# Four feed-forward gemms begun with half-token products, their first weights summed and split in the output projection, norm sums on VectorE

## The chip, the cores and the metric

One core of one Trainium2 chip runs the whole program. The metric is the device time of one execution in microseconds, as the median of several executions; lower is better. The profile is one execution of the same program, with its own time.

## The reference

One decoder layer over 1024 tokens of width 1024, in float32. After three token mixers (not touched here) it does

```python
x = x + mixed @ w_out                      # output projection
h = rms_norm(x, norm2_g)
ff = silu(h @ w_gate) * (h @ w_up)         # 1024 -> 2816, twice
x = x + ff @ w_down                        # 2816 -> 1024
x = x + sigmoid(x @ ple_gate) * (p @ ple_proj)
return rms_norm(x, final_g)
```

`rms_norm` divides each token by the root of its mean square, so h of a token is known only when all 1024 outputs of the output projection are known for that token.

## The kernel before, in words

Activations lie transposed: features on the 128 partitions, 512 tokens (a half) along the free axis. A "unit" is a tile of 128x512. Every float32 product is made of three TensorE products: each operand is split into a rounded high part (a copy on ScalarE, `act.copy`) and a rest (a subtraction on VectorE), and hi·hi, hi·lo and lo·hi are summed in PSUM.

**Output projection** (loop before the feed forward): for each token half `hf`, eight gemms of 24 matmuls; `out_evac` adds the residual on VectorE, squares on ScalarE, and sums the squares on VectorE. `norm2(hf)` follows its half: matmuls with a column of ones (`rstd`), a power on GpSimd, a matmul that spreads the result over the partitions (`rows`), then `normed` scales the eight units. `norm2(0)` runs beside the gemms of the second half; `norm2(1)` can begin only after the last gemm.

**Feed forward.** 22 gemms (gate and up for each of 11 pairs of 128-feature blocks), each by the Winograd form of Strassen's scheme: the output is 2 feature blocks x 2 token halves, and seven products of 12 matmuls stand in for eight. The token operands of the seven are B[0] to B[6]. B[0] and B[1] are the split normed units of the first half. B[2] to B[6] need the second half: per k of four, `T1 = t12 - ts0`, `T2 = t22 - T1`, B[2] = T2, B[3] = t22 - t12, B[4] = T1, B[5] = t22, B[6] = t21 - T2. In `norm2` the subtractions of T1 and T2 stand on VectorE, those of B[3] and B[6] on GpSimd; each B unit is then split by `b_split` (one copy on ScalarE, one subtraction on VectorE). The B units stay on the chip for all 22 gemms. The weight operands are sums of four blocks (`pool.tensor_tensor`, four per gemm, on GpSimd), split by `act.copy` and `vec.tensor_tensor` in `weights()`.

The order within a gemm is fixed in `Gemm`: `head1` (product 0, into bank X, then copied to p1 by ScalarE), `head2` (product 1), `middle` (products 2, 3, 4; X is copied as u after product 2 and as v after product 4 by ScalarE, and product 4 waits until u is read), `tail1` (product 5 on top of X, which waits until v is read), `tail2` (product 6). The heads of the next gemm are put between the tails of the current one. `op_slots` lets six split weight operands be ready ahead; two gemms' raw weights are held (`raw_slots`), in `stg` and in `ffp`, and `down_sums` has two tiles "dr" of its own for the down projection's weights, which it sums on GpSimd and stores.

`weights()` is started at the last-but-one gemm of the output projection (`j == KT - 2`).

**Down projection.** 77 steps of 12 matmuls; `d_load` loads two units a step, four steps ahead (`d_slots`), and `d_split` splits both. They are started after the last feed-forward gemm has been issued.

**What sets the order.** All engines execute their instructions in program order. `Flow` is a planner in Python: it keeps an estimated clock, advanced by the matmuls issued (`fl.tick`), and generators started with `fl.spawn` issue their instructions when their estimated due time comes. A wait (`yield`, `Event`, `Slots`) in the planner decides where an instruction stands in its engine's queue; on the chip the instruction waits for its data and for its buffer only. GpSimd's cost in the planner does not depend on what VectorE does, and VectorE's not on GpSimd.

Of the kernel before, what the change touches and what calls it, by code (L numbers as in the profile page):

```python
# [9 lines left out]
F32 = mybir.dt.float32  # L10
# [6 lines left out]
P = 128  # L17
S = 1024
HALF = 512
D = 1024  # L20
# [175 lines left out]
def kernel(  # L196
# [1020 lines left out]

    B = [[None] * 4 for _ in range(7)]
    B_ev = [[Event(fl) for _ in range(4)] for _ in range(7)]

    def b_split(i, k, t, sub):
        hi, lo = B[i][k] = unit(F32R), unit(F32R)
# [5 lines left out]
    def norm2(hf, ts):  # L1228
# [19 lines left out]
        for k in range(4):  # L1248
            t12, t22 = normed(k), normed(4 + k)
            T1[k], T2[k] = unit(), unit()  # L1250
            vec.tensor_tensor(out=T1[k], in0=t12, in1=ts[0][k], op=ALU.subtract)
            yield fl.lag("vec")
            vec.tensor_tensor(out=T2[k], in0=t22, in1=T1[k], op=ALU.subtract)
            ts[0][k] = None
            fl.spawn(b_split(2, k, T2[k], vec), fl.left())
            yield fl.lag("vec")
        for k in range(4):
            t = ts[1][k]
            pool.tensor_tensor(out=t, in0=ts[1][4 + k], in1=t, op=ALU.subtract)
            fl.spawn(b_split(3, k, t, vec), fl.left())  # L1260
            ts[1][k] = None
            yield 0.7
        for k in range(4):
            fl.spawn(b_split(4, k, T1[k], vec))
            T1[k] = None
            yield 1.3
        for k in range(4):
            t = ts[0][4 + k]
            pool.tensor_tensor(out=t, in0=t, in1=T2[k], op=ALU.subtract)
            fl.spawn(b_split(5, k, ts[1][4 + k], vec))  # L1270
            T2[k] = ts[1][4 + k] = None
            yield 1.3
        for k in range(4):
            fl.spawn(b_split(6, k, ts[0][4 + k], vec))
            ts[0][4 + k] = None
            yield 1.3

# [4 lines left out]
    jobs = []  # L1282
    for p in range(NPR):
        jobs += [(w_gate[2 * p], w_gate[2 * p + 1]), (w_up[2 * p], w_up[2 * p + 1])]
    ops, op_free = [], []
    op_slots, raw_slots = Slots(fl, 6), Slots(fl, 2)
    op_n = [0]

    def op_tile():
        n = op_n[0] % 6  # L1290
        op_n[0] += 1
        hp, tag = ((stg, "wh"), (stg, "wl"), (ffp, "op"))[n % 3]
        t = hp.tile([P, 8, P], F32R, tag=tag, name=nm("op"))
        return t[:, 0:4], t[:, 4:8]

    def weights():
        loaded = []

        def loader():
            for sa, sb in jobs:  # L1300
                yield from raw_slots.take()
                ra = stg.tile([P, KT, P], F32, tag="wr", name=nm("wr"))
                rb = ffp.tile([P, KT, P], F32, tag="wr", name=nm("wr"))
                ev = Event(fl)
                sync.dma_start(out=rb, in_=sb)
                sync.dma_start(out=ra, in_=sa)
                loaded.append((ra, rb, ev))
                ev.set(3.6)
                more.append(0)
                if waiting:  # L1310
                    waiting.pop().set()
                yield 0.1

        more, waiting = [], []
        fl.spawn(loader())
        own = []

        uses = [(0, 0), (0, 1)]
        for n in range(len(jobs)):
            uses += [(n, 2), (n, 3), (n, 4), (n + 1, 0), (n, 5), (n + 1, 1), (n, 6)]  # L1320
        for n, i in uses:
            if n == len(jobs):
                continue
            if n == len(own):
                if not more:
                    waiting.append(Event(fl))
                    yield waiting[-1]
                more.pop()
                ra, rb, ev = loaded.pop(0)
                yield ev  # L1330
                a11, a12, a21, a22 = ra[:, 0:4], ra[:, 4:8], rb[:, 0:4], rb[:, 4:8]
                s1 = unit(shape=(P, 4, P))
                pool.tensor_tensor(out=s1, in0=a21, in1=a22, op=ALU.add)
                pool.tensor_tensor(out=a21, in0=a11, in1=a21, op=ALU.subtract)
                own.append((a11, a12, a11, a21, s1, a12, a22))
                ra = rb = s1 = None
            yield from op_slots.take()
            a11, a12, s2, s3, s1, s4, a22 = own[n]
            if i == 2:
                pool.tensor_tensor(out=s2, in0=s1, in1=a11, op=ALU.subtract)  # L1340
                pool.tensor_tensor(out=s4, in0=a12, in1=s2, op=ALU.subtract)
            raw = own[n][i]
# [3 lines left out]
            ops.append((hi, lo))  # L1346
            if op_free:
                op_free.pop().set()
            if i == 6:
                own[n] = None  # L1350
                raw_slots.give()
            yield 0.3

    def next_op():
# [15 lines left out]


    class Gemm:
        def __init__(self, done):
            self.done = done

            self.read = {n: Event(fl) for n in ("p1", "u", "v", "y")}

# [10 lines left out]
        def middle(self):  # L1388
            fl.until(self.read["p1"])
            product(self.X, 2, False, True)  # L1390
            fl.spawn(self.snap("u"), 0.3)
            self.Y = bank(True)
            product(self.Y, 3, True, True)
            fl.until(self.read["u"])
            product(self.X, 4, False, True)
            fl.spawn(self.c22(), 0.3)

        def tail1(self):
            fl.until(self.read["v"])
            product(self.X, 5, False, True)  # L1400
            fl.spawn(self.done(self.X, None, 0, 1), 0.3)

        def tail2(self):
            fl.until(self.read["y"])
# [3 lines left out]
        def snap(self, name):  # L1408
            t = unit()
            setattr(self, name, t)  # L1410
            act.copy(out=t, in_=self.X)
            self.read[name].set()
            yield 0

# [57 lines left out]

    def down_sums(p):

        da, db = (ffp.tile([P, D], F32, tag="dr", name=nm("dr")) for _ in range(2))
        sync.dma_start(out=da, in_=w_down[2 * p])
        sync.dma_start(out=db, in_=w_down[2 * p + 1])
        s1 = unit()
# [6 lines left out]
        yield fl.lag("pool")  # L1485
        for i, t in enumerate((a11, a21, s1, a12)):
            sync.dma_start(out=wd_d[i, p], in_=t)

    xl_load(0)
    ts2 = [[None] * KT, [None] * KT]  # L1490
    for hf in range(2):
# [15 lines left out]
    todo = []  # L1507
    for p in range(NPR):
        ts, ev = [[None, None], [None, None]], Event(fl, 4)
        todo += [(p, Gemm(gate_done(ts)), None), (p, Gemm(up_done(ts, ev)), (ts, ev))]  # L1510
    todo[0][1].head1()
    todo[0][1].head2()
    for n, (p, g, ab) in enumerate(todo):
        g.middle()
        nxt = todo[n + 1][1] if n + 1 < len(todo) else None
        if nxt:
            nxt.head1()
        g.tail1()
        if nxt:
            nxt.head2()  # L1520
        g.tail2()
        if ab:
            fl.spawn(a_sums(p, *ab), 0.4)
        else:
            fl.spawn(down_sums(p), 2.0)
    B = None

    x2 = [[None] * KT, [None] * KT]  # L1530
# [19 lines left out]
    def d_split():  # L1550
        for _ in steps_:
# [10 lines left out]
            if d_wait:  # L1562
                d_wait.pop().set()
            yield 0.3

    def down_evac(ps, j, hf, last, read):
        vec.tensor_tensor(out=x1[hf][j], in0=ps, in1=x1[hf][j], op=ALU.add)
# [36 lines left out]
            fl.tick(3 * T_R)  # L1604
        d_slots.give()

    fl.spawn(d_load())
    fl.spawn(d_split(), 0.1)
    fl.tick(0.6)
    ff.close()  # L1610
    wd = ctx.enter_context(tc.tile_pool(name="wd", bufs=4))
# [176 lines left out]
```

## Time and profile before

| | us |
|---|---|
| median of 3 runs | 1272.01 (1271.91 to 1272.81) |
| the profiled execution | 1270.8 |
| its span, first to last instruction | 1268.8 |
| TensorE busy | 1219.7 (96%) |
| VectorE busy | 796.7 (63%) |
| ScalarE busy | 522.0 (41%) |
| GpSimd busy | 326.8 (26%) |

In the profile, PE is TensorE's matmuls, DVE is VectorE, ACT ScalarE, POOL GpSimd, SP the queue that issues the DMAs. Busy shares are averages over stages that differ; the strip of 40 slices and the tables by stretch show where a stage departs from them. Tiles are named without numbers: `mm` and `dn` are PSUM banks, `u` a unit, `op` a split weight operand, `wr` raw weights, `dr` raw weights of the down projection, `x_d` and `a_d` scratch in DRAM.

### The profile page before, as it was taken

What the parts mean: (1) busy time and instruction counts of PE and PEld (TensorE: products, weight loads), DVE (VectorE), ACT (ScalarE), POOL (GpSimd) and SP (SyncE); (2) the same over time, 40 slices, a digit from 0 to 9 for tenths busy, and PEclk for the clock granted to TensorE, in tenths of its full rate; (3) what the DMA queues carried; (4) which work ended last, traced back from release to release, by engine and by line L of the source; (5) the groups of instructions that cost most, each with busy time, mean ns of one, the idle gap of its engine ahead of it and who ended that gap; (6) DMA issues with size and microseconds to landing.
All of it is one profiled execution on the core that took longest, in us unless ns stands there. A gap on an engine that the chain in (4) does not pass through costs nothing.

```text
span 1268.8 us, 17177 instructions
## 1 busy us (share of the span) xinstructions
PE 1219.7 (96%) x6151; PEld 1006.5 (79%) x6151; DVE 796.7 (63%) x1361; ACT 522.0 (41%) x1102; POOL 326.8 (26%) x265
## 2 busy tenths in 40 slices
PE   7999999999999994999999999999989999999996
PEld 5778888888877872788888888888867888888896
DVE  8674886975675678756555555654447555574573
ACT  7266344253244342433333333333326542454442
POOL 7100000100100025456666655666310000000000
PEclk9999999999999995899999999999999999999998
DMA  6056254232245551145345545345578565562241
GB/s 221 17 154 190 86 134 121 101 84 84 100 158 160 189 191 50 57 151 184 108 156 191 166 149 182 112 156 199 191 277 293 193 199 172 161 215 67 84 144 57
DMA packets 105157, 187.18 MB, mean 148 GB/s; under 512 B 22960, under 2 KB 34032, under 8 KB 105072
## 3 DMA queue, kind: packets, MB, share of 16 engines
q1 hardware_dynamic: 105072, 186.09, 45.0%
q8 instruction: 48, 0.79, 0.3%
q14 instruction: 37, 0.30, 0.1%
HBM read 135.95 MB, written 50.10 MB: 147 GB/s over the span
## 4 chain that ended last, share of the span: by engine, by line
PE 62%; DVE 4%; DMA 2%; ACT 1%; issue 1%; POOL 0%; SPq 0%; POOLq 0%; DVEq 0%; ACTq 0%
PE dn L346 40%; PE mm L346 22%; DVE u L140 4%; ACT u L140 1%; DMA u<-x_d 1%; DMA u<-in_w_down_dram 1%; DVE op L140 1%; DMA a_d<-u 0%; DVE wl L140 0%; ACT op L140 0%; ACT wh L140 0%; SPq L240 0%; POOL rs L140 0%; POOL wr L140 0%; POOLq L1783 0%
## 5 line engine op out<-in xcount | busy, mean ns | idle before, releaser
L346 PE MATMUL dn<-u,op 128*128 128x512 f32 x1584 | 374.8, 396 | 16.6 <-DVE u L140 9.0
L346 PEld LDWEIGHTS dn<-u,op 128*128 128x128 f32 x1584 | 300.8, 191 | 88.1 <-DVE u L140 14.7
L346 PE MATMUL mm<-u,wh 128*128 128x512 f32 x1104 | 352.2, 400 | 7.5 <-DVE u L140 6.0
L346 PEld LDWEIGHTS mm<-u,wh 128*128 128x128 f32 x1104 | 201.3, 189 | 50.9 <-DVE u L140 8.4
L140 DVE TENSOR_TENSOR u<-u,u 128x512 fp32r<-128x512 f32 (+2 forms) x330 | 219.1, 706 | 30.3 <-ACT u L140 24.2
L346 PE MATMUL mm<-u,wl 128*128 128x512 f32 x552 | 216.1, 391 | 0.2 <-DVE wl L140 0.2
L140 DVE TENSOR_TENSOR op<-wr,op 128x512 fp32r<-128x512 f32 x132 | 139.4, 1059 | 117.4 <-ACT op L140 116.9
L140 ACT CAST u<-u 128x512 fp32r<-128x512 f32 x218 | 126.0, 619 | 145.7 <-DVE u L140 72.7
L346 PE MATMUL dn<-u,u 128*128 128x512 f32 (+2 forms) x850 | 161.7, 338 | 5.9 <-DVE u L140 4.9
L346 PEld LDWEIGHTS dn<-u,u 128*128 128x128 f32 (+1 forms) x850 | 124.5, 171 | 31.4 <-DVE u L140 5.6
L140 ACT CAST op<-wr 128x512 fp32r<-128x512 f32 x132 | 81.8, 621 | 155.2 <-POOL wr L140 58.1
L346 PE MATMUL mm<-u,u 128*128 128x512 f32 (+1 forms) x618 | 123.7, 340 | 0.0
L140 POOL TENSOR_TENSOR u<-u,u 128x512 f32<-128x512 f32 (+1 forms) x69 | 99.2, 1452 | 88.8 <-DVE u L140 80.7
L346 PEld LDWEIGHTS mm<-u,wl 128*128 128x128 f32 x552 | 103.8, 188 | 23.0 <-DVE wl L140 1.0
L140 ACT ACTIVATE u<-u 128x512 f32<-128x512 f32 (+1 forms) x137 | 82.1, 605 | 78.8 <-DVE u L140 77.0
L140 DVE TENSOR_TENSOR wl<-wr,wh 128x512 fp32r<-128x512 f32 (+2 forms) x96 | 68.3, 714 | 69.4 <-ACT wh L140 68.8
L140 POOL TENSOR_TENSOR rs<-ms,mhalf 128x4 f32<-128x4 f32 (+1 forms) x7 | 6.5, 926 | 399.4 <-DVE ms L140 399.4
L346 PEld LDWEIGHTS mm<-u,u 128*128 128x128 f32 x618 | 97.4, 190 | 13.4 <-ACT u L140 0.2
L140 ACT COPY u<-dn 128x512 f32<-128x512 f32 (+4 forms) x107 | 52.4, 490 | 129.6 <-PE dn L346 129.6
L140 DVE TENSOR_TENSOR u<-dn,u 128x512 f32<-128x512 f32 x81 | 55.6, 688 | 63.7 <-PE dn L346 53.1
L140 DVE TENSOR_TENSOR u<-mm,u 128x512 f32<-128x512 f32 x64 | 43.9, 687 | 56.5 <-PE mm L346 56.5
L140 ACT CAST wh<-wr 128x512 fp32r<-128x512 f32 (+2 forms) x96 | 57.6, 607 | 24.0 <-PE mm L346 11.7
(166 smaller groups left out, 1170.1 us busy)
## 6 DMA issues: line engine op xcount, KB each, us to landing
a_d<-u SPq DMA_DIRECT2D x77, 256.0 KB, 6.1
u<-a_d SPq DMA_DIRECT2D x77, 256.0 KB, 3.3
wr<-in_w_gate_dram SPq DMA_DIRECT2D x22, 512.0 KB, 4.4
wr<-in_w_up_dram SPq DMA_DIRECT2D x22, 512.0 KB, 4.6
dr<-in_w_down_dram SPq DMA_DIRECT2D x22, 512.0 KB, 6.1
u<-wd_d SPq DMA_DIRECT2D x44, 256.0 KB, 2.7
wr<-in_w_in_dram SPq DMA_DIRECT2D x21, 512.0 KB, 3.6
wd_d<-dr SPq DMA_DIRECT2D x33, 256.0 KB, 6.0
```

What stands on the lines that cost most here:

```text
L140: return f(*a, **kw)
L346: pe.matmul(out=out, lhsT=lhsT, rhs=rhs, start=start, stop=stop, **kw)
```

## The change

- `EARLY = 4`: the first four gemms (gate and up of the first two pairs) are taken in two pairs. First come products 0 and 1 of all four, then products 2 to 6 of gemms 0 and 1 in turn, then of gemms 2 and 3. The others keep their order.
- An early gemm adds product 1 onto product 0 in the same bank X and evacuates it at once; it begins X anew with product 2, and adds p1 when it reads X: u and v become additions on VectorE (before: copies on ScalarE), and the last read of X has an addition more.
- `weights()` starts at gemm `j == 1` of the second half of the output projection. The first four operands have tiles in `ffp`; the next ones take the tiles of the output projection's weights, after `out_w` at `j == KT - 2`. Eight operand tiles then (before: six). Sums are a generator of their own per gemm. The operands 2 to 6 of a gemm wait in the planner for `t2_ev`, set when the last T2 has been issued.
- The second raw tile of a gemm and the two tiles of `down_sums` come from one set of four (before: two and two).
- The subtractions of B[3] and B[6] go from GpSimd to VectorE, in order B[2], B[3], B[4], B[5], B[6], each loop pacing itself by VectorE's queue.
- The store of x1 is planned 3 us later; `d_load` and `d_split` are started before the last gemm (before: after it).

```diff
-        yield fl.left()
+        yield fl.left() + 3.0
         sync.dma_start(out=x1_d[hf, j], in_=x)
...
+        t2_ev.set()
         for k in range(4):
             t = ts[1][k]
-            pool.tensor_tensor(out=t, in0=ts[1][4 + k], in1=t, op=ALU.subtract)
+            vec.tensor_tensor(out=t, in0=ts[1][4 + k], in1=t, op=ALU.subtract)
             fl.spawn(b_split(3, k, t, vec), fl.left())
...
         for k in range(4):
             t = ts[0][4 + k]
-            pool.tensor_tensor(out=t, in0=t, in1=T2[k], op=ALU.subtract)
-            fl.spawn(b_split(5, k, ts[1][4 + k], vec))
+            vec.tensor_tensor(out=t, in0=t, in1=T2[k], op=ALU.subtract)
+            fl.spawn(b_split(6, k, t, vec), fl.left())
...
+    EARLY = 4
+    uses = []
+    for n in range(0, EARLY, 2):
+        uses += [(n, 0), (n + 1, 0), (n, 1), (n + 1, 1)]
+    for n in range(0, EARLY, 2):
+        uses += [(n + b, i) for i in range(2, 7) for b in range(2)]
...
-    op_slots, raw_slots = Slots(fl, 6), Slots(fl, 2)
+    op_slots, ra_slots, rb_slots, out_w = Slots(fl, 4), Slots(fl, 2), Slots(fl, 4), Event(fl)
...
+            todo = [(n, c) for n in range(2) for c in range(2)] + [(2, 0), (3, 0), (2, 1), (3, 1)]
+            todo += [(n, c) for n in range(4, len(jobs)) for c in range(2)]
+            for n, c in todo:
+                if n >= 2 and c == 0:
+                    yield out_w
+                    yield from ra_slots.take()
+                else:
+                    yield from rb_slots.take()
+                fetch(n, c)
...
+                if i == 2:
+                    yield t2_ev
+                yield sum_ev[n]
...
         def head2(self):
+            if self.early:
+                fl.until(self.read["p1"])
+                product(self.X, 1, False, True)
+                fl.spawn(self.done(self.X, None, 0, 0), 0.3)
+                return
...
+            if self.early and name != "p1":
+                vec.tensor_tensor(out=t, in0=self.X, in1=self.p1, op=ALU.add)
+            else:
+                act.copy(out=t, in_=self.X)
...
-        da, db = (ffp.tile([P, D], F32, tag="dr", name=nm("dr")) for _ in range(2))
+        yield from rb_slots.take()
+        yield from rb_slots.take()
+        da, db = (raw_tile(ffp).rearrange("p k c -> p (k c)") for _ in range(2))
...
-            if hf == 1 and j == KT - 2:
+            if hf == 1 and j == 1:
                 fl.spawn(weights())
...
+            if hf == 1 and j == KT - 2:
+                out_w.set()
+                for _ in range(4):
+                    op_slots.give()
...
+    for n in range(0, EARLY, 2):
+        for f in (Gemm.head1, Gemm.head2):
+            f(g[n])
+            f(g[n + 1])
+    for n in range(0, EARLY, 2):
+        for f in (Gemm.p6, Gemm.p7, Gemm.p5, Gemm.tail1, Gemm.tail2):
+            f(g[n])
+            f(g[n + 1])
...
+        if not nxt:
+            fl.spawn(d_load())
+            fl.spawn(d_split(), 0.1)
```

In the new code `p6`, `p7` and `p5` are products 2, 3 and 4, the three parts of the old `middle`.

## Rows read from the trace of the kernel before

**Rows 1.** The page's strip of 40 slices: busy tenths, and the granted clock
```profile
PE   7999999999999994999999999999989999999996
PEclk9999999999999995899999999999999999999998
```

**Rows 2.** Table by stretch: busy us (instructions) of each engine, granted clock, DMA share
```profile
468.10:540.05 71.95, 51.02 (x170) 34.93 (x170) 54.80 (x67) 26.35 (x48) 33.95 (x23) 0.74 0.17 59
500.00:510.00 10.00, 5.74 (x12) 2.67 (x11) 9.06 (x8) 4.22 (x8) 8.69 (x7) 0.50 0.57 210
516.00:517.00 1.00, 1.00 (x6) 0.81 (x5) 0.00 (x0) 0.94 (x2) 0.00 (x0) 1.00 0.00 0
600.00:700.00 100.00, 100.00 (x443) 82.81 (x442) 54.83 (x64) 36.56 (x64) 59.81 (x43) 1.00 0.46 155
```

**Rows 3.** Timeline of PE: start, us, count, [idle before <-releaser]
```profile
468.16 2.88 PE L346 MATMUL dn<-u,op 128*128 128x512 f32 x12
470.88 2.88 PE L346 MATMUL mm<-u,op 128*128 128x512 f32 x12
476.46 1.02 PE L346 MATMUL dn<-ones,u 128*128 128x1 f32 x8 [2.70 <-DVE u L140]
479.83 2.04 PE L346 MATMUL dn<-u,ones 128*128 128x512 f32 x2 [2.35 <-DVE u L140]
485.40 0.77 PE L346 MATMUL dn<-u,op 128*128 128x512 f32 x1 [3.52 <-issue]
...
503.57 3.33 PE L346 MATMUL dn<-u,op 128*128 128x512 f32 x6 [2.95 <-DVE u L140]
```

**Rows 4.** Timeline of DVE over the same stretch
```profile
467.22 1.23 DVE L140 TENSOR_TENSOR op<-wr,op 128x512 fp32r<-128x512 f32 x1 [1.83 <-ACT op L140]
...
472.65 0.68 DVE L140 TENSOR_TENSOR u<-mm,u 128x512 f32<-128x512 f32 x1
...
481.92 1.41 DVE L140 SCALAR_TENSOR_TENSOR u<-u,vt,dn 128x512 f32<-128x512 f32 x2 [2.23 <-PE dn L346]
...
501.75 9.69 DVE L140 TENSOR_TENSOR u<-u,u 128x512 fp32r<-128x512 f32 x7
...
512.39 1.89 DVE L140 TENSOR_TENSOR u<-u,u 128x512 fp32r<-128x512 f32 x3
```

**Rows 5.** Table by stretch: the output projection of the second half
```profile
424.00:468.10 44.10, 44.10 (x198) 36.30 (x197) 30.92 (x51) 17.63 (x31) 6.70 (x6) 1.00 0.63 209
```

**Rows 6.** Groups by line and form, 545 to 900 us: count | busy, mean ns
```profile
L140 DVE TENSOR_TENSOR op<-wr,op 128x512 fp32r<-128x512 f32 x113 | 121.5, 1077 | 100.7 <-ACT op L140 100.2
L140 DVE TENSOR_TENSOR u<-dn,u 128x512 f32<-128x512 f32 x46 | 31.6, 687 | 18.3 <-PE dn L346 18.0
L140 POOL TENSOR_TENSOR wr<-wr 128x512 f32<-128x512 f32 x19 | 24.5, 1292 | 1.5
```

**Rows 7.** Timeline of PE at the entry of the down projection
```profile
928.99 3.58 PE L346 MATMUL dn<-u,u 128*128 128x512 f32 x8 [4.67 <-DVE u L140]
...
953.35 0.50 PE L346 MATMUL dn<-u,u 128*128 128x512 f32 x1 [1.02 <-ACT u L140]
```

**Rows 8.** Timeline of DVE there
```profile
924.13 0.69 DVE L140 TENSOR_TENSOR u<-dn,u 128x512 f32<-128x512 f32 x1 [2.03 <-PE dn L346]
924.85 7.69 DVE L140 TENSOR_TENSOR u<-u,u 128x512 f32<-128x512 f32 x9
```

**Rows 9.** Table by stretch, after that entry
```profile
930.00:940.00 10.00, 10.00 (x41) 8.13 (x40) 3.87 (x7) 1.24 (x2) 0.00 (x0) 0.89 0.99 352
940.00:950.00 10.00, 10.00 (x46) 8.29 (x45) 4.05 (x6) 3.63 (x6) 0.00 (x0) 1.00 1.05 385
```

**Rows 10.** The page's DMA issues: count, KB, us from issue to landing
```profile
wr<-in_w_gate_dram SPq DMA_DIRECT2D x22, 512.0 KB, 4.4
dr<-in_w_down_dram SPq DMA_DIRECT2D x22, 512.0 KB, 6.1
wd_d<-dr SPq DMA_DIRECT2D x33, 256.0 KB, 6.0
```

More of the change, by code (lines that the diff above doesn't have):

```diff
@@ L1284 @@
         jobs += [(w_gate[2 * p], w_gate[2 * p + 1]), (w_up[2 * p], w_up[2 * p + 1])]
+    EARLY = 4
[4 more added lines that the diff above has]
+        uses += [(n + b, i) for i in range(2, 7) for b in range(2)]
+    uses += [(EARLY, 0), (EARLY, 1)]
+    for n in range(EARLY, len(jobs)):
+        more = n + 1 < len(jobs)
+        uses += [(n, 2), (n, 3), (n, 4)] + [(n + 1, 0)] * more + [(n, 5)] + [(n + 1, 1)] * more + [(n, 6)]
@@ L1294, in op_tile, with raw_tile @@
         return t[:, 0:4], t[:, 4:8]
+    def raw_tile(hp):
+        return hp.tile([P, KT, P], F32, tag="wr", name=nm("wr"), bufs=2 if hp is stg else 4)
     def weights():
-        loaded = []
-        def loader():
[L1300 to L1311, printed above, removed]
-                yield 0.1
@@ L1314, in weights, with fetch @@
-        more, waiting = [], []
+        raws = [[None, None, Event(fl), Event(fl)] for _ in jobs]
+        def fetch(n, c):
+            raws[n][c] = raw_tile(ffp if c or n < 2 else stg)
+            sync.dma_start(out=raws[n][c], in_=jobs[n][c])
+            raws[n][2 + c].set(3.6)
+        def loader():
+            todo = [(n, c) for n in range(2) for c in range(2)] + [(2, 0), (3, 0), (2, 1), (3, 1)]
[7 more added lines that the diff above has]
+                fetch(n, c)
+                yield 0.1
@@ new lines, in sums @@
+        def sums(n):
+            yield raws[n][2]
+            yield raws[n][3]
+            ra, rb = raws[n][0:2]
+            a11, a12, a21, a22 = ra[:, 0:4], ra[:, 4:8], rb[:, 0:4], rb[:, 4:8]
+            s1 = unit(shape=(P, 4, P))
+            pool.tensor_tensor(out=s1, in0=a21, in1=a22, op=ALU.add)
+            pool.tensor_tensor(out=a21, in0=a11, in1=a21, op=ALU.subtract)
+            own[n] = (a11, a12, a11, a21, s1, a12, a22)
+            yield split_ev[n]
+            pool.tensor_tensor(out=a11, in0=s1, in1=a11, op=ALU.subtract)
+            pool.tensor_tensor(out=a12, in0=a12, in1=a11, op=ALU.subtract)
+            sum_ev[n].set()
@@ L1315, in weights @@
+        own = [None] * len(jobs)
+        split_ev, sum_ev = events(len(jobs)), events(len(jobs))
         fl.spawn(loader())
[L1316 to L1320, printed above, removed]
+        started = 0
         for n, i in uses:
[L1322 to L1336, printed above, removed]
-            yield from op_slots.take()
[L1338 to L1342, printed above, removed]
@@ L1343, in weights @@
+            while started < len(jobs) and started <= n + 1:
+                fl.spawn(sums(started))
+                started += 1
+            yield from op_slots.take()
+            if i < 2:
+                yield raws[n][2]
+                raw = raws[n][0][:, 4 * i:4 * i + 4]
+            else:
+                if i == 2:
+                    yield t2_ev
+                yield sum_ev[n]
+                raw = own[n][i]
             hi, lo = op_tile()
@@ L1346, in weights @@
             ops.append((hi, lo))
+            if i == 1:
+                split_ev[n].set()
             if op_free:
@@ L1349, in weights @@
             if i == 6:
-                own[n] = None
-                raw_slots.give()
+                own[n] = raws[n] = raw = None
+                (rb_slots if n < 2 else ra_slots).give()
+                rb_slots.give()
             yield 0.3
@@ L1372, with __init__ @@
     class Gemm:
-        def __init__(self, done):
-            self.done = done
+        def __init__(self, done, early=False):
+            self.done, self.early = done, early
             self.read = {n: Event(fl) for n in ("p1", "u", "v", "y")}
@@ L1386, in head2, with p6, p7, p5 @@
             fl.spawn(self.c11(), 0.3)
-        def middle(self):
+        def p6(self):
             fl.until(self.read["p1"])
-            product(self.X, 2, False, True)
+            if self.early:
+                self.X = bank(True)
+            product(self.X, 2, self.early, True)
             fl.spawn(self.snap("u"), 0.3)
+        def p7(self):
             self.Y = bank(True)
             product(self.Y, 3, True, True)
+        def p5(self):
             fl.until(self.read["u"])
@@ L1400, in tail1 @@
             product(self.X, 5, False, True)
-            fl.spawn(self.done(self.X, None, 0, 1), 0.3)
+            fl.spawn(self.done(self.X, self.p1 if self.early else None, 0, 1), 0.3)
         def tail2(self):
@@ L1410, in snap @@
             setattr(self, name, t)
-            act.copy(out=t, in_=self.X)
+            if self.early and name != "p1":
+                vec.tensor_tensor(out=t, in0=self.X, in1=self.p1, op=ALU.add)
+            else:
+                act.copy(out=t, in_=self.X)
             self.read[name].set()
@@ L1487, in down_sums @@
             sync.dma_start(out=wd_d[i, p], in_=t)
+        rb_slots.give()
+        rb_slots.give()
     xl_load(0)
@@ L1564, in d_split, with after @@
             yield 0.3
+    todo = []
+    for p in range(NPR):
+        ts, ev = [[None, None], [None, None]], Event(fl, 4)
+        early = 2 * p < EARLY
+        todo += [(p, Gemm(gate_done(ts), early), None), (p, Gemm(up_done(ts, ev), early), (ts, ev))]
+    def after(n):
+        p, _, ab = todo[n]
+        if ab:
+            fl.spawn(a_sums(p, *ab), 0.4)
+        else:
+            fl.spawn(down_sums(p), 2.0)
+    g = [t[1] for t in todo]
+    for n in range(0, EARLY, 2):
[6 more added lines that the diff above has]
+            f(g[n + 1])
+        after(n)
+        after(n + 1)
+    g[EARLY].head1()
+    g[EARLY].head2()
+    for n in range(EARLY, len(g)):
+        nxt = g[n + 1] if n + 1 < len(g) else None
+        if not nxt:
+            fl.spawn(d_load())
+            fl.spawn(d_split(), 0.1)
+        g[n].p6()
+        g[n].p7()
+        g[n].p5()
+        if nxt:
+            nxt.head1()
+        g[n].tail1()
+        if nxt:
+            nxt.head2()
+        g[n].tail2()
+        after(n)
+    B = None
     def down_evac(ps, j, hf, last, read):
@@ L1605, in down_step @@
         d_slots.give()
-    fl.spawn(d_load())
-    fl.spawn(d_split(), 0.1)
     fl.tick(0.6)
```

43 lines of the change are left out of this document (12 added, 31 removed).

## The prediction, made before the changed kernel was run

> **What bounds the kernel now.** I read the page's strip first. TensorE is at nine tenths or more nearly everywhere, so a gain can come only from slices where it is not. The deepest inner one is slice 15 (476 to 507 us), the entry of the feed forward, and there the granted clock falls too; a shallower one is slice 29, the entry of the down projection [rows 1]. The first slice and the last are not touched by the change.
>
> Next the table by stretch. A saturated feed forward runs 443 matmuls in 100 us, 0.2257 us each, with VectorE at 55% and GpSimd at 60%: more work on either there costs nothing as long as TensorE is not kept waiting. From 468.10 (the end of the output projection) to 540.05, where TensorE has been back at that pace for 12 us, 71.95 us hold 170 matmuls, 10 of them the norm's. The other 160 are worth 36.1 us, so **35.8 us are lost here**, part of it to waiting and part to the clock, which stands at 0.50, the 1.2 GHz level, in 500 to 510 and is back at 1.00 only by 516 [rows 2].
>
> The timeline of TensorE shows why. Two half-token products (2.72 us from start to start) are all it has; then come the norm's matmuls at 476.46 and 479.83, the first matmul that needs the second half at 485.40, and B[3] at 503.57 [rows 3]. VectorE's timeline names the delays. At 467.22 it sits in its queue behind a weight split that waits for ScalarE (itself late for GpSimd's sums), so the last gemm, done at about 468.4, is evacuated only at 472.65. The scaling begins at 481.92. Subtractions of two SBUF operands take 9.69 us for 7 (one per 1.4 us) in 501 to 511 while GpSimd is 87% busy, against 1.89 us for 3 (0.605 from start to start) when it is idle [rows 2, 4].
>
> **The change part by part.**
>
> *Six more half-token products.* Eight products of 2.72 us keep TensorE busy for 21.7 us after 468.2, plus the norm's matmuls: 2.0 us at full clock (1.02 and half of the 2.04, which ran at half clock [rows 3]). With 1.5 us for the norm's two waits (bounds 0 and the 5.1 of the two idle times in rows 3), product 2 could start at 493.4.
>
> *When B[2] is there.* With the first sums and splits moved some 30 us earlier, the last evacuation no longer stands behind them: 468.4 instead of 472.65, and the norm's first matmul follows at about 471, not 476.46 (evacuation, square and sum, 0.7 us each, and one split in between). From that matmul to the first scaling it took 5.46 us (476.46 to 481.92), so scaling starts at 476.5. Four times two scalings (1.32) and three subtractions (0.605 each, GpSimd idle) are 12.5 us; one evacuation between (0.69) and two of the four late weight splits bring the last T2 to 491. The first operand of product 2 is split behind it: 492.5. So TensorE, not the norm, is last here, or nearly so; I take product 2 at 494 and 0.6 us of waiting, bounds 0 and 5 (the norm chain of before kept, 4.2 us later). Queued behind that wait is all of TensorE's later work.
>
> *The sums moved into the output projection.* There TensorE never waits, VectorE is busy 30.9 of 44.1 us and GpSimd 6.7 [rows 5]. Four splits (2.4 us; three of them stood there already) and four more GpSimd sums fit under the gemms: 0. Raw weights land in 4.4 us [rows 10], with DMA at 0.63. If the cover were gone (VectorE late for the weights of the next gemm), it would cost up to 2 us. The later x1 store holds only a buffer longer; behind it on SP stand the loads of the early weights, needed tens of us later: 0.
>
> *The two pairs.* Every B stage now feeds two products, 5.4 us of TensorE. From 491 to the use of the last B[6] tile (494 + 8 products 21.7 + 2 = 518) VectorE has 27 us. Its work: 24 instructions for B[3] to B[6] (8 subtractions, now its own, and 16 splits), 10 weight splits, all 0.605, and 10 evacuations and snapshots at 0.687 [rows 6]: 20.6 + 6.9 = 27.5. Beside it GpSimd makes the eight sums of gemms 2 and 3, since their second raw tiles can land only after the sixth operand of gemms 0 and 1 is split (slots), at about 503. A VectorE instruction beside GpSimd took 1.45 us on average against 0.605, 0.85 more; eight of them, 6.8. So VectorE needs 34.3 us for 27: **7.3 us of waiting**, spread over B[4] to B[6]. Bounds: 0, if the sums fall where VectorE has evacuations from PSUM, and 14. The moved subtractions add 8 x 0.605 = 4.8 us to VectorE and spare it 8 x 0.85 = 6.8 of waiting behind GpSimd; the copies taken from ScalarE gain nothing, as ScalarE is not last. Gemms 2 and 3 find all of B there: 0.5 (0 to 3).
>
> Lost after: 2.0 + 1.5 + 0.6 + 7.3 + 0.5 = 11.9. Gain at this entry 35.8 - 11.9 = **23.9** (bounds 13 and 33).
>
> *Down projection.* TensorE stands 4.67 us at its entry, since the splits of the first steps lie in VectorE's queue behind the last evacuation at 924.13 [rows 7, 8], and then has 41 matmuls in 10 us instead of 44.3 (clock 0.89), 0.75 us more [rows 9]. With `d_load` and `d_split` before the last gemm the splits lie beside that gemm: up to 5.4 us gained. But DMA is at 0.99 to 1.05 for the 20 us behind, and already made step 8 wait at 953.35; a TensorE that starts sooner gets there sooner. I take **3**, bounds 0 and 6. The added risk: a copy that waits for a landing stands ahead of the last gemm's snapshots on ScalarE.
>
> *The rest.* Eight operand tiles and the shared raw tiles: 0 in a saturated stretch (priced as a rival below).
>
> **Sum.** 1270.8 (span 1268.8 and 2.0 around it) - 23.9 - 3.0 = 1243.9. The median of before is 1.2 above its profiled execution, so the forecast is **1245**, its own range 1238 to 1254.
>
> **Where a page bears on it.** VectorE's splits (both inputs in SBUF) average 1.077 us in the feed forward, its evacuations from PSUM 0.687, beside the same GpSimd [rows 6]. The Trainium skill, page "SBUF — State Buffer", section "Who interferes with whom", says that a VectorE instruction with two SBUF inputs and a GpSimd instruction that reads SBUF exclude each other for the whole instruction, while one with a single SBUF input is not disturbed. The trace agrees in kind. By that rule each of the eight sums could hold VectorE for its full length, and the moved subtractions are put on the engine that is held; this is worked out from rows as rival A.
>
> **Rivals.**
>
> *A: VectorE becomes the bound and the clock falls again.* The eight sums cost VectorE their whole 1.292 us [rows 6], 10.3 instead of 6.8; TensorE, fed a tile at a time, drops to 0.50 as it did around 500 to 510 [rows 2], and some 30 matmuls at half clock cost 0.2257 more each, 6.8. The gain at the down projection is eaten by DMA, 3.0. Together 13.3: 1258. For it: the same feeding by tiles before. Against: TensorE has 21.7 us of full work just ahead and two products per stage.
>
> *B: no stall in the pairs.* The sums find VectorE in evacuations or come after the B stages: 7.3 less, and the down projection gives 5: 1236. Against: VectorE's own 27.5 us already fill its 27.
>
> *C: the raw tiles become the wait (slower).* `down_sums` now takes two of four tiles that gemms need for the second half of their weights. It holds them for the load (6.1), four sums (5.2 to 6.5) and the stores (6.0), some 18 us of a pair's 38 [rows 6, 10]. If a gemm's load came last behind these stores, the nine later pairs would each wait. It turns slower from 27 / 9 = 3 us a pair; at 4 us it is 1245 + 36 = 1281. Against: two gemms hold two tiles for about 20 us each, so 4 x 38 = 152 tile-us face 2 x 18 + 2 x 20 = 76.
>
> *D: the change does not cover what it means to.* The norm's matmuls are placed too early among the half-token products and TensorE waits there instead, or the operands of gemms 2 and 3 come late: the wait of before moves, and only the 4.3 us of the earlier evacuation remain: 1268.
>
> **How the numbers follow.** Forecast 0.56, A 0.20, B 0.13, C 0.06, D 0.05. The range of 8 in 10 takes in B with a little below it and A with a little above: 1234 to 1260; that leaves out C, D and the tails. What a measurement can tell from no change is 0.2%, 2.5 us: faster is all but C, and a part of D, 0.92; same 0.02; slower 0.06.
>
> **What would show it.** TensorE's timeline after the last output gemm: eight runs of 12 matmuls with the norm's matmuls among them and idle times under 2 us each; the norm's first matmul near 471; product 2 at 493 to 495; the granted clock at 1.00 (2.4 GHz) from 468 to 530. Waits for VectorE's units of B[4] to B[6], 5 to 10 us in all, beside GpSimd's sums. The idle time before the first down step under 1 us, and a longer wait for the DMA some steps later. 443 matmuls per 100 us in the rest of the feed forward. It is wrong if TensorE still stands more than 5 us for the norm, if the clock falls, or if idle time appears between 560 and 900.

## The result and the profile after

The changed kernel takes **1259.05 us** (1255.54 to 1259.93, 4 runs) against 1271.96 before: ratio 0.9892, 95% interval 0.9873 to 0.9912. A second group gave 1258.5 (1258.02 to 1261.25), ratio 0.9909 (0.9894 to 0.9925). It is 1.1% faster, clear of the noise. The time lies inside the stated range of 1234 to 1260 but at its slow end, and outside the forecast's own range of 1238 to 1254: 12.9 us gained where 27 were forecast.

The page of the profile after, whose span is 1253.8 us (the fastest run): busy tenths in 40 slices, and the granted clock. The hole of slice 15 [rows 1] has become a shallow one in slice 16; the clock still dips, and one slice later.

```profile
PE   8999999999999999799999999999999999999996
PEclk9999999999999999899999999999999999999998
```

The timeline of TensorE at the entry of the feed forward answers to [rows 3].

```profile
470.57 4.92 PE L346 MATMUL dn<-u,op 128*128 128x512 f32 x21
476.86 1.02 PE L346 MATMUL dn<-ones,u 128*128 128x1 f32 x8 [1.37 <-DVE u L140]
477.74 3.03 PE L346 MATMUL dn<-u,op 128*128 128x512 f32 x12
480.61 1.02 PE L346 MATMUL dn<-u,ones 128*128 128x512 f32 x2
481.07 21.46 PE L346 MATMUL dn<-u,op 128*128 128x512 f32 x91
504.15 0.97 PE L346 MATMUL dn<-u,op 128*128 128x512 f32 x3 [1.62 <-DVE u L140]
507.75 7.95 PE L346 MATMUL dn<-u,op 128*128 128x512 f32 x27 [2.64 <-DVE u L140]
517.63 5.07 PE L346 MATMUL dn<-u,op 128*128 128x512 f32 x14 [1.93 <-DVE u L140]
525.21 9.31 PE L346 MATMUL dn<-u,op 128*128 128x512 f32 x34 [2.50 <-ACT u L140]
535.33 22.52 PE L346 MATMUL dn<-u,op 128*128 128x512 f32 x98 [0.81 <-DVE u L140]
559.57 11.16 PE L346 MATMUL dn<-u,op 128*128 128x512 f32 x48 [1.72 <-ACT u L140]
```

The half-token products do what was said: from 470.57 on, 124 matmuls (21, 12 and 91) run with one wait of 1.37 us and without a drop of the clock. The 96 of the heads end at 481.07 + 63 x 0.2267 = 495.4 (0.2267 is 2.72 us divided by 12), product 2 follows with no wait, and the first wait for B comes behind 502.5, in B[3]. The norm itself does not come as early as forecast: ScalarE's half of a weight split waits 2.30 us for its landing, VectorE's half waits for ScalarE, and the last evacuation stands behind it.

```profile
471.66 0.62 ACT L140 CAST op<-wr 128x512 fp32r<-128x512 f32 x1 [2.30 <-DMA wr<-in_w_up_dram]
```
```profile
472.32 0.69 DVE L140 TENSOR_TENSOR op<-wr,op 128x512 fp32r<-128x512 f32 x1 [2.14 <-ACT op L140]
472.93 0.68 DVE L140 TENSOR_TENSOR u<-mm,u 128x512 f32<-128x512 f32 x1
```

What fails in the feed forward begins behind 502.5. The table by stretch (columns as in rows 2) shows that, and a loss ahead of it: the output projection of the second half, from its norm's first matmul to the first half-token product; the covered stretch; and the pairs, where 99 matmuls ran in 37.5 us that could hold 166, at a mean clock of 0.86.

```profile
425.44:470.57 45.13, 42.75 (x183) 32.60 (x181) 35.38 (x51) 17.77 (x32) 13.23 (x9) 1.00 0.60 203
470.57:502.50 31.93, 30.56 (x135) 24.18 (x133) 24.42 (x43) 14.48 (x26) 1.02 (x1) 1.00 0.07 27
502.50:540.00 37.50, 28.00 (x99) 21.32 (x99) 31.61 (x44) 14.42 (x25) 18.43 (x11) 0.86 0.18 63
```

The first of these stretches was all TensorE work before [rows 5]; the timeline of TensorE now shows waits for the output projection's own weights (`wl`), of which these are the longest. (TensorE's idle time in the stretch is 45.13 - 42.75 = 2.4 us; the rest of what it lost lies in shorter delays between matmuls that the timeline does not list as waits.)

```profile
444.57 0.50 PE L346 MATMUL mm<-u,wl 128*128 128x512 f32 x1 [1.53 <-DVE wl L140]
448.13 0.50 PE L346 MATMUL mm<-u,wl 128*128 128x512 f32 x1 [0.55 <-DVE wl L140]
```

The lines of three other engines name what B[4] and the units after it waited for: ScalarE's split of a weight of gemm 2 waits 4.70 us for GpSimd, VectorE's half of that split 4.56 us for ScalarE, and the first sum on GpSimd took 4.17 us. The splits of B stand behind in both queues. Then VectorE is slowed: 5.11 us for three of its instructions, beside sums of 1.6 to 1.7 us each.

```profile
514.01 0.63 ACT L140 CAST op<-wr 128x512 fp32r<-128x512 f32 x1 [4.70 <-POOL wr L140]
```
```profile
506.41 3.70 DVE L140 TENSOR_TENSOR u<-u,u 128x512 f32<-128x512 f32 x6
...
514.67 1.24 DVE L140 TENSOR_TENSOR op<-wr,op 128x512 fp32r<-128x512 f32 x1 [4.56 <-ACT op L140]
515.83 5.11 DVE L140 TENSOR_TENSOR u<-u,u 128x512 fp32r<-128x512 f32 x3
```
```profile
507.08 4.17 POOL L140 TENSOR_TENSOR u<-wr 128x512 f32<-128x512 f32 x1 [27.90 <-DVE op L140]
...
517.11 1.60 POOL L140 TENSOR_TENSOR wr<-wr,wr 128x512 f32<-128x512 f32 x1
```

The wait of 1.72 us at 559.57 is of another kind. By the counts above, 300 of the 336 matmuls of the four early gemms have run by then, so it stands before product 5 of gemm 3. The chain back from it goes through an evacuation on VectorE that stands behind the split of a weight of gemm 4, which waits for GpSimd's sums.

```profile
556.33 0.63 ACT L140 CAST op<-wr 128x512 fp32r<-128x512 f32 x1 [5.98 <-POOL wr L140]
```
```profile
556.99 1.23 DVE L140 TENSOR_TENSOR op<-wr,op 128x512 fp32r<-128x512 f32 x1 [3.79 <-ACT op L140]
```

At the entry of the down projection the 4.67 us of [rows 7] are gone: the first of its matmuls, at 911.54, follows the last product without idle time. The wait further on has grown from 1.02 to 1.93 us, with DMA at 1.02 to 1.04 and the clock at 0.83 in the next 10 us.

```profile
905.96 5.74 PE L346 MATMUL dn<-u,op 128*128 128x512 f32 x24 [0.68 <-ACT u L140]
911.54 2.20 PE L346 MATMUL dn<-u,u 128*128 128x512 f32 x9
930.22 0.50 PE L346 MATMUL dn<-u,u 128*128 128x512 f32 x1 [1.93 <-ACT u L140]
```

**Stage by stage.** The time at which a run reaches the norm of the first half differs from profile to profile by up to 7 us (425.4 to 432.5), which says nothing of the change. So I measure three stretches of each profiled execution between TensorE's own instructions: *out*, from the first norm matmul of half 0 to the first half-token product (183 matmuls before and after); *ff*, from there to the end of the last feed-forward product; *rest*, to the end of the span. 1848 matmuls at 0.2257 make 417.1 us of *ff* at the least. The two profiles of the changed kernel agree within 0.3 us in each. The runs were made in groups, on several chips, and the kernel before ran in each: its medians were 1269.83 to 1271.96, so a difference of 2 us between medians of different groups says nothing.

| kernel | out | ff | rest | median us |
|---|---|---|---|---|
| before | 40.6 | 455.9 | 344.7 | 1271.96 |
| changed, first group | 45.1 | 441.1 | 342.1 | 1259.05 |
| changed, in the second group | 45.4 | 441.4 | 342.1 | 1258.5 |
| e1 sums waiting in the planner | 45.7 | 442.9 | 342.2 | 1258.37 |
| e1b weights from gemm 4 | 49.1 | 440.4 | 341.7 | 1261.21 |
| e9 second raw tiles later | 42.7 | 445.5 | 341.4 | 1258.14 |
| e2 sums counted as later | 45.0 | 442.8 | 341.6 | 1259.47 |
| e3 splits of 2, 3 after B | 45.8 | 440.7 | 342.6 | 1259.45 |
| e7 splits in step with B | 45.2 | 447.9 | 341.9 | 1267.52 |
| e8 six raw tiles | 45.4 | 451.3 | 341.9 | 1267.07 |
| c89 e8 and e9 | 43.7 | 452.9 | 341.6 | 1266.91 |
| e4 norm sums on GpSimd | 45.2 | 446.7 | 342.9 | 1263.93 |
| e6 no early gemms | 42.9 | 450.5 | 341.6 | 1264.46 |
| e10 no sums for gemms 2, 3 | 45.3 | 433.0 | 341.8 | 1250.67 |

The change gains 14.8 in *ff* and 2.6 in *rest* and loses 4.5 in *out*: 12.9. The forecast had 23.9, 3.0 and 0, so of the 14.0 that are missing 9.1 lie in *ff*, 4.5 in *out* and 0.4 in *rest*.

One thing in *ff* differs from profile to profile without an edit that was meant to do it: the clock beside the norm. In e1, e2 and e9 the 12 matmuls behind the norm's first matmuls took 4.25, 4.49 and 5.47 us, against 2.99 to 3.03 in the changed kernel. So 1.3 to 2.5 us of their *ff* is clock lost there.

### The profile page after: what moved, and what is told of

It is laid out like the page before. It is cut to its first block, busy times and chain, and to the rows that moved or that the text cites. A ratio compares the mean times of both kernels' runs of the same rounds, so it can differ in the third digit from the quotient of the medians.

```text
span 1253.8 us, 17171 instructions
## 1 busy us (share of the span) xinstructions
PE 1215.4 (97%) x6151; PEld 1003.6 (80%) x6151; DVE 794.6 (63%) x1377; ACT 518.1 (41%) x1094; POOL 317.5 (25%) x257
## 4 chain that ended last, share of the span: by engine, by line
PE 58%; DVE 6%; DMA 2%; ACT 2%; issue 1%; POOL 1%; SPq 0%; POOLq 0%; DVEq 0%; ACTq 0%
PE dn L346 38%; PE mm L346 20%; DVE u L140 4%; DMA wr<-in_w_up_dram 1%; ACT u L140 1%; DVE op L140 1%; DVE wl L140 1%; POOL wr L140 1%; POOL u L140 1%; DMA u<-x_d 1%; DMA u<-in_w_down_dram 0%; ACT op L140 0%; ACT wh L140 0%; POOLq L1849 0%; SPq L1319 0%
## 5 line engine op out<-in xcount | busy, mean ns | idle before, releaser
L346 PE MATMUL dn<-u,op 128*128 128x512 f32 x1632 | 380.6, 393 | 11.9 <-DVE u L140 7.0
L346 PEld LDWEIGHTS dn<-u,op 128*128 128x128 f32 x1632 | 308.7, 190 | 80.2 <-DVE u L140 9.0
L140 DVE TENSOR_TENSOR u<-u,u 128x512 fp32r<-128x512 f32 (+2 forms) x338 | 229.3, 723 | 42.1 <-ACT u L140 37.6
L140 DVE TENSOR_TENSOR op<-wr,op 128x512 fp32r<-128x512 f32 x132 | 123.0, 934 | 101.9 <-ACT op L140 100.1
L140 ACT COPY u<-dn 128x512 f32<-128x512 f32 (+4 forms) x99 | 47.8, 482 | 139.6 <-PE dn L346 138.0
L140 POOL TENSOR_TENSOR u<-u,u 128x512 f32<-128x512 f32 (+1 forms) x61 | 92.6, 1532 | 38.7 <-DVE u L140 27.4
L140 DVE TENSOR_TENSOR u<-dn,u 128x512 f32<-128x512 f32 x93 | 63.6, 688 | 60.9 <-PE dn L346 52.7
L140 DVE TENSOR_TENSOR u<-mm,u 128x512 f32<-128x512 f32 x60 | 41.2, 687 | 56.2 <-PE mm L346 53.2
```

Source lines behind the costliest of these rows:

```text
L140: return f(*a, **kw)
L346: pe.matmul(out=out, lhsT=lhsT, rhs=rhs, start=start, stop=stop, **kw)
```

## The experiments

Each edit is made to the changed kernel; the medians stand in the table.

**The reference again.**

> The changed kernel itself again, as the reference of this group: 1259 within 2, since its four runs lay between 1255.5 and 1259.9.

1258.5, as expected.

**No early gemms.**
```diff
-    EARLY = 4
+    EARLY = 0
```


> No gemm begun early (EARLY = 0), all the rest of the change kept. Theory: the six half-token products are the cover of the norm, 16.3 us of work; without them TensorE stands for the norm again: 1270 to 1276. Rival: most of the gain comes from the norm's sums on VectorE and the earlier weights: 1262 or less.

1264.46, between the two: both theories miss. The cover is worth 9.1 us of *ff* and costs 2.5 of *out*, 6 us together; the other half of the gain is the rest of the change. TensorE does stand again (10.24 us before product 2, 7.05 within product 3, for B[3]), but the norm itself comes 3.2 us earlier without the four late weight splits (3.4 us after the first half-token product, not 6.6).

**What the output projection loses.** Three tries.
```diff
+            if n < 2:
+                yield late_w        # e1: in sums(); set at gemm 5
```


> The eight GpSimd sums of gemms 0 and 1 wait for gemm 5 of the output projection; loads and splits stay early. Theory: VectorE, slowed beside these sums while it scales the first half, was late for the output projection's own weights, and that cost the output projection 4.7 us; so that stretch gets 3 to 5 us shorter, about 1255. Rival: the earlier loads or splits themselves delay it: 1259, the same stretch as long.

*out* stayed at 45.7, and GpSimd ran its sums from 433.45 to 446.3. That begins 7.9 us after the norm's first matmul, and 7.6 in the changed kernel: GpSimd had nothing else in its queue, so a later place in program order delayed nothing. The edit did not do what it was for and tells nothing of either theory.

```diff
-            if hf == 1 and j == 1:
+            if hf == 1 and j == 4:
                 fl.spawn(weights())
```


> The weights of the feed forward are started at gemm 4 of the output projection (the change: gemm 1; before: gemm 6). Theory: loads, splits and sums beside the scaling of the first half make VectorE late for the output projection's own weights, 4.6 us; from the norm's first matmul of half 0 to the first half-token product it takes 41 to 42 us instead of 45.2, and the whole gets 2 to 4 us faster, 1255. Rival: what the output projection gains is lost at the norm of the second half, since its evacuation stands behind these splits again: 1258.5 within 1.

Neither: *out* got longer, 49.1, with waits of 1.19, 2.46 and 1.24 us in the last gemm but one, and a clock of 0.73 from the second of them to the end of the stretch. The same work over fewer gemms costs more, so starting later is no cure.

```diff
-            todo = [(n, c) for n in range(2) for c in range(2)] + [(2, 0), (3, 0), (2, 1), (3, 1)]
+            todo = [(n, c) for c in range(2) for n in range(2)] + [(2, 0), (3, 0), (2, 1), (3, 1)]
...
+                    if n < 2 and c == 1:
+                        yield late_w       # e9: the load itself; set at gemm 4
                     yield from rb_slots.take()
```


> The second raw tiles of gemms 0 and 1 are loaded at gemm 4 of the output projection, so that the eight sums on GpSimd come after the scaling of the first half; first tiles and their splits stay at gemm 1. Theory: the sums hold VectorE beside that scaling, and with that the output projection's own weights; from the first norm matmul of half 0 to the first half-token product 42 us or less instead of 45.2. Rival: the four early splits, not the sums, cost it: 45.

*out* fell to 42.7, nearer to the theory than to the rival: the sums beside the scaling of the first half are 2.7 of the 4.8 us (45.4 - 40.6), and the rest belongs to the splits or to what the sums still disturb. But GpSimd now sums until 471, into the norm of the second half, and *ff* grows by 4.1: TensorE waits 2.66 us there instead of 1.67, and the next 12 matmuls take 5.47 us instead of 2.99, at a clock of 0.53 (timeline of TensorE). The median does not differ from the changed kernel's.

```profile
477.22 1.69 PE L346 MATMUL dn<-ones,u 128*128 128x1 f32 x8 [2.66 <-DVE u L140]
478.76 5.47 PE L346 MATMUL dn<-u,op 128*128 128x512 f32 x12
```

**What the pairs wait for.** First the order in the queues.
```diff
-            sum_ev[n].set()
+            sum_ev[n].set(fl.left() + 4.0 if n in (2, 3) else 0.0)
```


> The planner sees the sums of gemms 2 and 3 as ready only when GpSimd's queue has done them and 4 us more, so that their splits stand later in the queues of ScalarE and VectorE. Theory (queue): in the pairs stage these splits waited at the head of both queues for GpSimd, 4.6 us and more at a time, with the splits of B behind them; then the waits of TensorE between 502 and 560 us shrink by 6 to 10 us, 1249 to 1253. Rival (throughput, the forecast's own): VectorE has more work than time there, and the order in the queue changes nothing: 1259 within 2.

No gain: the number is the rival's. The timelines of GpSimd and of VectorE in this run say why: with the weight splits out of the way, 13 B instructions ran on VectorE without a gap, 0.605 us each, and the first sum lasted 8.15 us beside them. The weight split then waited at the head of the queue all the same, only later. (Of this run's *ff*, 1.5 us are the clock beside the norm.)

```profile
510.82 8.15 POOL L140 TENSOR_TENSOR u<-wr 128x512 f32<-128x512 f32 x1 [29.60 <-DVE u L140]
```
```profile
509.91 7.92 DVE L140 TENSOR_TENSOR u<-u,u 128x512 f32<-128x512 f32 x13
...
522.41 1.23 DVE L140 TENSOR_TENSOR op<-wr,op 128x512 fp32r<-128x512 f32 x1 [4.58 <-ACT op L140]
```

```diff
+                if n in (2, 3) and i == 2:
+                    yield st_ev[6]        # e3: set when all of B has been issued
```


> The splits of gemms 2 and 3 (operands 2 to 6) are issued only when all of B has been issued, so nothing that waits for GpSimd's late sums stands ahead of B in ScalarE's and VectorE's queues. Theory (queue): the idle 4 to 5 us of VectorE inside the pairs stage go, and the feed forward (first half-token product to its end, 441.3) takes 433 to 437: 1251 to 1255. Rival (supply): the sums themselves come too late, since the second raw tiles land late and GpSimd is held off while VectorE runs without a gap; then the wait only moves to product 2 of gemm 2: 440 or more, 1258.5 within 2.

The rival's number: *ff* 440.7. But the wait did not move to product 2 of gemm 2. The two waits for B[3] stay (1.63 and 2.65), those of 1.9 and 2.5 us behind them go, and two others grow: 3.39 us at 528.82, where 180 matmuls have run, so before product 5 of gemm 1, and 3.13 at 561.05, before product 5 of gemm 3. The first waits for an evacuation on VectorE that stands behind splits of B slowed by the sums (4.55 us for 3 instructions), the second for one behind the split of a weight of gemm 4, as in the changed kernel.

```diff
+                if n < 4:                 # e7
+                    k = 6 if n > 1 else i
+                    if k > 2:
+                        yield st_ev[k]    # set when B[k] has been issued
```


> As the run before, and the splits of gemms 0 and 1 follow B step by step (operand i is split only after B[i] has been issued) instead of running eight ahead. Theory: the waits of 1.6 and 2.6 us for B[3] go too, because eight weight splits no longer stand before it on VectorE: 430 to 435 for the feed forward, 1249 to 1253. Rival (supply): the sixth operand of gemms 0 and 1 is split later, so the raw tiles of gemms 2 and 3 land later still, and the feed forward takes 441 or more.

Worse, as the rival had it, by 6.5 in *ff*. B[3] is no longer waited for; 70 matmuls run nearly through. But the raw tiles of the later gemms come free later: the first sum of gemm 2 runs at 530.55, not 507.08. Product 5 of gemm 3 stands 6.91 us (timeline of TensorE), again behind the split of a weight of gemm 4, which waits 10.01 us for GpSimd on ScalarE.

```profile
510.73 18.20 PE L346 MATMUL dn<-u,op 128*128 128x512 f32 x70 [1.24 <-DVE op L140]
...
570.95 13.70 PE L346 MATMUL dn<-u,op 128*128 128x512 f32 x48 [6.91 <-ACT u L140]
```

Then the supply, with two more tiles.
```diff
-        return hp.tile([P, KT, P], F32, tag="wr", name=nm("wr"), bufs=2 if hp is stg else 4)
+        return hp.tile([P, KT, P], F32, tag="wr", name=nm("wr"), bufs=2 if hp is stg else 6)
...
-    ..., rb_slots, out_w = Slots(fl, 4), Slots(fl, 2), Slots(fl, 4), Event(fl)
+    ..., rb_slots, out_w = Slots(fl, 4), Slots(fl, 2), Slots(fl, 6), Event(fl)
```


> Six tiles for second raw weights instead of four, so that those of gemms 2 and 3 land during the output projection's end and not after the sixth operand of gemms 0 and 1 is split. Theory (supply): the late sums of gemms 2 to 4 are what the pairs stage and gemm 4 waited for, wherever their splits stood; the feed forward takes 428 to 434 instead of 441.3 and the whole 1247 to 1252. Rival (VectorE's throughput, the forecast's own): the eight sums now run beside the norm's scaling and hold VectorE there; product 2 starts later by what is gained: 439 or more, 1258.5 within 2.

Slower, and mainly for a reason that neither had: GpSimd's timeline shows the eight sums of gemms 2 and 3 one after the other from 475.06, and the norm's power (`rs`) behind them in the same queue. Its input was ready at 481.6; it ran at 486.66. VectorE's next step of the norm stood behind an evacuation until 490.01, and the norm's second matmul came at 491.85, 19.6 us after the first half-token product and not 10.3 as in the changed kernel. Only 36 of the 96 half-token matmuls were left behind it as cover, and product 2 waited 2.67 and 2.42 us for its weights. VectorE beside the sums, the rival's reason, accounts for part: the norm's first matmul came 1.5 us later.

```profile
475.06 1.30 POOL L140 TENSOR_TENSOR u<-wr 128x512 f32<-128x512 f32 x1 [27.73 <-issue]
...
485.42 1.29 POOL L140 TENSOR_TENSOR wr<-wr 128x512 f32<-128x512 f32 x1
486.66 1.02 POOL L140 TENSOR_TENSOR rs<-ms,mhalf 128x4 f32<-128x4 f32 x1
```

> Both edits. By the theories 10 to 13 us less than the changed kernel, 1246 to 1250; if the sums of all four gemms now crowd into the end of the output projection and the norm, 1255 to 1260.

Neither: as e8, and what *out* gains against e8 (1.7) *ff* loses (1.6). Six tiles with the sums placed behind that power were not tried.

**The sums by themselves.** The eight sums of gemms 2 and 3 are left out, with nothing else edited (unsummed blocks stand in, so this part of the computation is not the reference's).
```diff
+            if n in (2, 3):
+                own[n] = (a11, a12, a11, a21, a22, a12, a22)
+                yield split_ev[n]
+                sum_ev[n].set()
+                return
```


> The eight GpSimd sums of gemms 2 and 3 are left out (their products use unsummed blocks, so that output is not the reference's); loads, splits, slots and order stay. Theory: these sums, placed anywhere, are what VectorE and ScalarE wait for or share the port with in the pairs stage; without them the waits of TensorE between 505 and 538 us fall from 9.3 to 5 or less, the clock stays at 1.00 there, and the feed forward takes 428 to 433 instead of 441.3. Rival: VectorE's own work and its order (weight splits ahead of B[3]) is the bound, and the sums only fill its gaps: 437 or more.

As the theory had it, at its edge: *ff* 433.0, 8.4 less, and 1250.67. TensorE's waits between 505 and 538 fall from 9.3 to 5.1, and the mean clock from 502 to 540 rises from 0.87 to 0.96 (rows by stretch of this run; the timeline of TensorE below).

```profile
507.00 0.97 PE L346 MATMUL dn<-u,op 128*128 128x512 f32 x3 [1.62 <-DVE u L140]
510.61 18.84 PE L346 MATMUL dn<-u,op 128*128 128x512 f32 x75 [2.64 <-DVE u L140]
530.29 22.50 PE L346 MATMUL dn<-u,op 128*128 128x512 f32 x98 [0.84 <-DVE u L140]
```
```profile
502.00:540.00 38.00, 32.89 (x136) 25.89 (x136) 34.47 (x55) 17.84 (x32) 7.46 (x6) 0.96 0.26 85
510.00:515.00 5.00, 4.39 (x13) 3.44 (x14) 4.11 (x7) 3.83 (x7) 0.00 (x0) 0.66 0.91 328
```

The clock was not held throughout: it fell to 0.66 in 510 to 515, right after the two waits for B[3], which are the same as in the changed kernel. Those belong to VectorE's own work: ten weight splits stand on it between 495.58 and 506.41 in the changed kernel, ahead of B[3] and among its first splits, and in e7, which moves these, the two waits are gone.

**The norm sums.** B[3] and B[6] subtracted on GpSimd again.
```diff
-            vec.tensor_tensor(out=t, in0=ts[1][4 + k], in1=t, op=ALU.subtract)
+            pool.tensor_tensor(out=t, in0=ts[1][4 + k], in1=t, op=ALU.subtract)
...
-            vec.tensor_tensor(out=t, in0=t, in1=T2[k], op=ALU.subtract)
+            pool.tensor_tensor(out=t, in0=t, in1=T2[k], op=ALU.subtract)
```


> The subtractions of B[3] and B[6] go back to GpSimd, all else as changed. The forecast's own price: 4.8 us off VectorE, 6.8 us of contention on it: 2 us slower, 1260.5. Rival: VectorE is the bound and GpSimd idle there, so it gets 3 to 5 us faster; or, GpSimd being held off by a gapless VectorE, B[3] comes several us later and it is 1263 or more.

The third case by its number: 1263.93, *ff* 5.3 longer, with one wait of 7.59 us in the pairs (timeline of TensorE) where the changed kernel has 2.64 at most. Not by its reason: B[3] is waited for by less than 1 us at a time, and the long wait is for B[4], whose split stands on VectorE behind two weight splits that wait 4.56 and 4.48 us for the sums of gemms 2 and 3. So the move is worth some 5 us, more than the 2.0 that the forecast's price gave.

```profile
524.90 14.13 PE L346 MATMUL dn<-u,op 128*128 128x512 f32 x48 [7.59 <-DVE u L140]
```

No version that computes the reference beat the changed kernel; e1, e2, e3 and e9 cannot be told from it.

## Why the prediction was right in its direction and half wrong in size

- *Six more half-token products, norm waits 1.5, product 2 at 494 with 0.6 of waiting.* Right: 1.37, 495.4 and none, although the reason given for an earlier norm was wrong. The norm's first matmul came at 476.86, not 471: the last evacuation still stood behind a weight split that waited for ScalarE and its landing (one of the four late operands). The cover hid that. In e6, which has no late operands there, the norm comes 3.2 us earlier.
- *The sums moved into the output projection: 0.* This step failed. It cost 4.5 us, over the bound of 2. The argument was one of totals (30.9 of 44.1 us busy), but GpSimd's eight sums (432.83 to 445.67) and the early splits all fall beside the scaling of the first half, where VectorE had no room: it ran without idle time from 434.39 to 449.9, and its instructions took up to 1.77 us there. e9 gives 2.7 of it to the sums; what the rest is, no run separates.
- *The two pairs: 7.3 us of waiting, at full clock.* The place was right, VectorE with the sums of gemms 2 and 3 beside it; the size was not. The waits between 502 and 536 are 1.62 + 2.64 + 1.93 + 2.50 + 0.81 = 9.5, and e10 prices the sums at 8.4 (forecast 6.8; from start to start the rows give 9.69 / 7 = 1.38 for an instruction beside GpSimd, not 1.45, and so 6.2). Only half of the 8.4 is the slowing that was forecast: some 4.3 us on four instructions (5.11 + 1.57 us where 0.605 each would do). About as much, 4.56, is VectorE standing idle behind a weight split whose sum is late. Two things were missing altogether. VectorE's order, the weight splits ahead of B[3]: 4.3 us of waits that e10 keeps, of which e7 turns 1.9 into waits for the weights. And the clock: 0.86 over 37.5 us is 10.5 us at 1.2 GHz, at most 5.2 us lost. *ff* lost 441.1 - 417.1 = 24.0; the forecast, from 455.9, left 455.9 - 417.1 - 23.9 = 14.9. By the forecast's own signs it was wrong in this: the clock fell.
- *Gemms 2 and 3: 0.5.* Too low, inside its bounds of 0 to 3: product 5 of gemm 3 waits 1.72, and 3.1 to 6.9 us in e2, e3 and e7. All of B is there, as was said; what stands in the way is the split of a weight of gemm 4, whose sums are late in each of these runs.
- *Down projection: 3.* Measured 2.6. Right as given: 4.67 gained at the door, part given back in a longer wait and a lower clock with DMA full.
- *Rivals.* A came nearest: 1258, with the clock falling (6.8, at most 5.2 measured) and the sums at 10.3 (8.4 by e10). Its third part, the down projection's gain lost, did not happen; the output projection lost that and more instead. That its total fits is in part luck, and the measured time lies within the stated range only because that range was drawn to take in A. B and D are out by the time; of C nothing is seen, no wait of TensorE stands between 571 and 905 us.
- *The Trainium skill on the shared port* (page "SBUF — State Buffer", section "Who interferes with whom"). VectorE and GpSimd do hold each other up, but only half as I priced it. Four of the eight sums met VectorE in turn, and VectorE was slowed, as forecast. The first met a gapless VectorE, which was not slowed, and GpSimd was held: 4.17 us for a sum, and 8.15 in e2. Then the engines that wait for the sum pay.

## What to carry to other kernels

Cover for a stall moves the limit to whatever feeds the covered work. Price the operand supply of the next stage (buffers that come free, the sums and splits behind them) as a chain of its own, not as a total of busy time on each engine. A total over 44 us does not show a shortage of 15; add up by the stretch in which the moved work will land. And a later place in program order delays nothing on an engine whose queue is empty: to move work there, move its data, and look at what then stands behind it, as the norm's power did in e8.

## What the runs showed of the hardware

- One GpSimd sum (1.29 us alone) lasted 8.15 us while VectorE ran 13 subtractions of two SBUF operands at 0.605 us each; from 515.8 to 522 us of the changed kernel the two alternated at 1.6 to 1.7 us each. What decides between the two, no run shows.
- The clock fell after two waits of 1.62 and 2.64 us only 3.6 us apart (0.66 over the next 5 us in e10), though TensorE had run without a break for over 20 us before.
- Behind a single wait of TensorE for the norm the clock fell in some runs and not in others of nearly the same wait: after 1.58, 1.46 and 2.66 us (e1, e2, e9) it was 0.76, 0.72 and 0.53 over the 6 to 7 us around it, and after 1.37 and 1.67 us (the two profiles of the changed kernel) and 1.50 (e4) it stayed at 1.00. The length of the wait alone does not tell.
